# Half of the output projection moved from the third stage into the first, with group 0's qkv, the bias vectors and the first key loads in another order

## The chip, the cores and the metric

The kernel runs on one core of a Trainium2 chip. The metric is the device time of one execution in microseconds (us); lower is better. Of each kernel there are timed executions and one more under the hardware profiler, whose trace is shown here.

## The reference, cut to what matters

One layer of a hybrid decoder for a prompt of 2048 tokens and a sample group of 64 (8 sequences of 8 new tokens). All arrays are float32.

```
proj  = rms_norm(x) @ w_in              # 1024 -> q | k | v | r | k | v | three low-rank inputs
att   = dilated_attention(q, k, v)      # 8 heads x 64; three strided key sets, position bias
rw    = rwkv7_time_mix(proj[..., 1536:])   # 8 heads x 64; a state of 64 x 64 per head, token after token
h     = x + concat([att, rw], -1) @ w_out          # 1024 -> 1024
y     = h + relu(rms_norm(h) @ w_mlp1)**2 @ w_mlp2 # 1024 -> 4096 -> 1024
```

The rows 0 to 511 of `w_out` belong to attention (A), the rows 512 to 1023 to the recurrence (R). The projection is a sum of both halves, so either can be added first. The sample group reads 2048 cached keys and values for each of its eight sequences.

## The kernel before, in words

Every product with weights is done as three matmuls of rounded halves (hi x hi, hi x lo, lo x hi), so each operand is split by ScalarE (hi) and VectorE (lo = value - hi) first (`split`). Partitions hold features, columns hold tokens. All DMAs are issued from SP, in one queue, in order.

The order of each engine's instructions is fixed when the program is built: a planner simulates the program and takes, among what it believes ready, what has the best priority. Text order is the priority, except inside `with urgent()`, which puts its instructions ahead of all filler.

**Stage one** (`ph1`). Tokens are taken in four groups of 512, the 64 sample tokens with group 0. `norm1(g)` writes the normalised group as eight tile pairs nh, nl (one buffer each). `proj(g)` makes the recurrence's 15 column blocks (`rproj`, matmuls at L330) and stores them to xsD; `qkv(g)` makes the attention's six blocks (matmuls at L789) and stores qhD, qlD, khD, klD and vD. The recurrence runs in units of 256 tokens, the sample first, then units 0 to 7 (`core(unit(u))`), all urgent: small matmuls, a triangular solve on POOL, round trips through DRAM, then eight dependent chunks. Units 2g and 2g+1 need proj(g). Each unit's results go to DRAM as mixR. qkv(0) comes last, after all units, with a second `norm1(0)`:

```
proj(0, *nhl)
...
    if g + 1 < NG:
        proj(g + 1, *norm1(g + 1))      # qkv(g + 1) inside
for _ in qkv(0, *norm1(0)):
    pass
```

`bias_vectors` builds the position bias in DRAM: bvD holds, for each head, the bias by distance repeated for 128 partitions. It is advanced by one step after each block of proj(1).

**Stage two.** Attention over four pairs of heads. `kq_load(p)` loads a pair's keys and queries in twelve DMAs of 64 partitions x 2048 columns, `bias_load` its bias, `next_v` the values. A pair's three branches are merged and stored to DRAM as mixA.

**Stage three.** For eight chunks of 264 tokens, the output projection: `wo_panel` loads and splits a panel of 128 rows of w_out, `mix_panel` 128 rows of mixA or mixR, and each of eight output blocks takes 24 matmuls (L1431), the recurrence's panels 4 to 7 first. The residual x is loaded into h (L1421) and the sum added. The sample's attention is interleaved, two steps after each output block: it streams 42 MB of cached keys and values through four buffers of 512 KB. Its results, attS, are columns of the last chunk.

**Stage four.** The MLP (L1488, L1505) in two halves of the tokens.

Of the kernel before, what the change touches and what calls it, by code (L numbers as in the profile page):

```python
# [9 lines left out]
F32 = mybir.dt.float32  # L10
F32R = mybir.dt.float32r
# [19 lines left out]
def bc(ap, axis, n):  # L31
    a = ap.unsqueeze(axis)
    shape = list(a.shape)
    shape[axis] = n
    return a.broadcast_to(shape)
# [135 lines left out]
def _build(ctx, tc, nc, I, O, dbg, upto):  # L171
# [8 lines left out]
    def tt(out, a, b, op):  # L180
        V.tensor_tensor(out, a, b, op)  # L181
# [37 lines left out]
    xsD = dram.tile([15, P, T + NS], F32, name="xsD")  # L219
    mixA = dram.tile([4, P, T + NS], F32, name="mixA")  # L220
    mixR = dram.tile([4, P, T + NS], F32, name="mixR")


    rw = ph1.enter_context(pool(name="rw", bufs=1))
# [27 lines left out]
    def pj():  # L252
        return ppj.tile([P, 512], F32, name="pj", tag="pj")

    def split(src, hi, lo):
        act(hi, src, AF.Copy)
        tt(lo, src, hi.bitcast(F32), ALU.subtract)
# [200 lines left out]
    def bias_vectors():  # L458

        btab = c1.tile([33, 8], F32, name="btab")  # L460
        nc.sync.dma_start(out=btab, in_=I["btab"])
        bv1 = dram.tile([8, 3, 384], F32, name="bv1")

        def by_distance(src, n):
            oh = wp.tile([P, 512], F32, name="oh", tag="qn", bufs=3)
            nc.sync.dma_start(out=oh[:33, :n], in_=src)
            ps = pj()
            PE.matmul(ps[:8, :n], btab, oh[:33, :n], start=True, stop=True)
            sb = wp.tile([P, 512], F32, name="sb", tag="qn", bufs=3)
            act(sb[:8, :n], ps[:8, :n], AF.Copy)  # L470
            return sb

        for b in range(3):
            nc.sync.dma_start(out=bv1[:, b], in_=by_distance(I["oneh"][:, b], 384)[:8, :384])
            yield
        for h in range(0, 8, 4):
            nc.sync.dma_start(out=bvD[h:h + 4].rearrange("h p b n -> h p (b n)"), in_=bc(bv1[h:h + 4].rearrange("h b n -> h (b n)"), 1, P))
        for c in range(0, NSV, 512):
            n = min(512, NSV - c)
            nc.sync.dma_start(out=svD[:, :, c:c + n], in_=bc(by_distance(I["soneh"][:, c:c + n], n)[:8, :n], 1, 8))  # L480
            yield
# [208 lines left out]
            urgent.at, tc.cur_priority = tc.cur_priority, self.other  # L690

    AFTER = ((), (), (), ())

    def proj(g, nh, nl):

        other = qkv(g, nh, nl) if g else iter(())
        for i, j in enumerate((12, 13, 14, 4, 0, 8, 5, 1, 9, 6, 2, 10, 7, 3, 11)):
            rproj(g, j, nh, nl)  # L700
            if g == 1:
                next(bias, None)
            if i in AFTER[g]:
                next(other, None)
            if i == 12 and g + 1 < NG:
                sums(g + 1)
        for _ in other:
            pass

    def unit(g):  # L710
        st = new_unit()
# [35 lines left out]
    def sample_unit():  # L747
        st = new_unit()

        def padded(js, t):  # L750
            n = len(range(*js.indices(15)))
            c = rw3.tile([P, 3, NS], F32, name="xsc", bufs=1)[:, :n]
            nc.sync.dma_start(out=c, in_=xsD[js, :, T:].rearrange("j q t -> q j t"))
            G.memset(t, 0.0)
            for j in range(n):
                G.tensor_copy(t[:, j].rearrange("p (b i) -> p b i", i=C)[:, :, :8], c[:, j].rearrange("p (b i) -> p b i", i=8))
            return t

        st["lora"] = lora_prep(lambda t: padded(slice(12, 13), t.unsqueeze(1)))

        def xgate():
            x = rw3.tile([P, 3, UT], F32, name="xrkv")
            nc.sync.dma_start(out=x[:, 0, :NS], in_=xsD[13, :, T:])
            nc.sync.dma_start(out=x[:32, 1, :NS], in_=xsD[14, :32, T:])
            return x[:, 0, :NS], x[:32, 1, :NS]

        st["xgate"] = xgate
        preps(st, lambda p: padded(slice(p, p + 9, 4), rw3.tile([P, 3, UT], F32, name="xrkv")), True)
        return st
# [171 lines left out]
    urgent.at, tc.cur_priority = tc.cur_priority, tc.cur_priority + FILL  # L941
    with urgent():
        core(sample_unit(), UT, True, -1, lambda n: None)
    z = zt[core.count % NZ]
    G.memset(z[0:64, 0], 0.0)
    G.memset(z[64:128, 1], 0.0)
    for g in range(NG):
        for u in (2 * g, 2 * g + 1):
            with urgent():
                core(unit(u), UT, False, u, lambda n: None)  # L950
        if g + 1 < NG:
            proj(g + 1, *norm1(g + 1))
            if g + 2 == NG:
                nc.sync.dma_start(out=O["o_shift"], in_=sho)
    for _ in qkv(0, *norm1(0)):
        pass
    prj.close()

    ph1.close()
# [31 lines left out]

    evac.n = 0

    def kq_load(p):

        kq = kqs[p % 2]
        K = []
        for ty in range(2):
            rr = slice(ty * 64, ty * 64 + 64)
            kst = kq.tile([P, T], F32R, name=f"kst{ty}", tag="kq")  # L1000
            klo = kq.tile([P, T], F32R, name=f"klo{ty}", tag="kq")
            qst = kq.tile([P, T], F32R, name=f"qst{ty}", tag="kq")
            for dst, src, r0 in ((kst, khD, 0), (qst, qhD, 0), (kst, khD, 64), (qst, qlD, 64), (klo, klD, 0), (klo, klD, 64)):
                nc.sync.dma_start(out=dst[r0:r0 + 64].bitcast(F32), in_=src[p, rr])
            K.append((kst, klo, qst))
        return K

    def bias_load(p, b):
# [171 lines left out]
                yield  # L1180
            nc.sync.dma_start(out=mixA[p, :, cs], in_=ob[0][:, cs])

    ahead = {("kq", 0): kq_load(0)}
    for b in range(3):
        ahead["bias", 0, b] = bias_load(0, b)
    vq.append(next(vgen))
    wsel = at.tile([P, 4, P], F32R, name="wsel")
    wsel0 = at.tile([P, 4, P], F32, name="wsel0", tag="pts", bufs=4)
    nc.sync.dma_start(out=wsel0, in_=I["wsel"])
# [102 lines left out]

    NT = T + NS
    NC_ = 264
    woh = [None] * KT
    wol = [None] * KT

    def wo_panel(w, k):

        woh[k], wol[k] = w[:, 0:D], w[:, D:]  # L1300
        for o in range(0, D, 512):
            wr = we.tile([P, 512], F32, name="raw", bufs=3)
            nc.sync.dma_start(out=wr, in_=I["wo"][:, k, o:o + 512])
            split(wr, woh[k][:, o:o + 512], wol[k][:, o:o + 512])

    def mix_panel(pl, k, c0):

        mh = pl.tile([P, NC_], F32R, name="mh", bufs=5)
        ml = pl.tile([P, NC_], F32R, name="ml", bufs=5)
        src = (mixA if k < 4 else mixR)[k % 4]  # L1310
        n = min(NC_, (T if k < 4 else NT) - c0)
        mr = we.tile([P, 512], F32, name="mr", tag="raw", bufs=3)
        nc.sync.dma_start(out=mr[:, :n], in_=src[:, c0:c0 + n])
        split(mr[:, :n], mh[:, :n], ml[:, :n])
        if n < NC_:
            split(attS[:, k], mh[:, n:], ml[:, n:])
        return mh, ml
# [37 lines left out]
    attS = sat.tile([P, 4, NS], F32, name="attS")  # L1355

    kvs.append((sat, 2))
    for k in (4, 5):
        wo_panel(we.tile([P, 2 * D], F32R, name=f"wo{k}"), k)
    mixed = {}  # L1360
    for k in range(4, 8):
        mixed[k, 0] = mix_panel(we, k, 0)
    for _ in rest:
        pass
    ph2.close()
# [43 lines left out]
    with pool(name="wo2", bufs=1) as wo2, pool(name="pwo", bufs=4, space=PSUM, side="right") as pwo, pool(name="psa", bufs=1, space=PSUM) as psa, pool(name="pst", bufs=1, space=PSUM) as pst:  # L1409
        kvs.append((wo2, 2))  # L1410
        sample = sample_all(psa)
        for k in (6, 7, 0, 1, 2, 3):
            wo_panel(kqb.tile([P, T], F32R, name="wo", tag="kq"), k)
        tile_ = 0
        ends = [(i + 1) * P for i in range(8)] + [1088 + i * P for i in range(9)]
        order = (4, 5, 6, 7, 0, 1, 2, 3)
        for c0 in range(0, NT, NC_):
            if c0 + NC_ == NT:
                for _ in sample:
                    pass  # L1420
            nc.sync.dma_start(out=h[:, :, c0:c0 + NC_], in_=I["xh"][:, :, c0:c0 + NC_])  # L1421
            for k in order:
                if (k, c0) not in mixed:
                    mixed[k, c0] = mix_panel(we if k >= 4 else wo2, k, c0)
            for o in range(KT):
                ps = pwo.tile([P, 512], F32, name="pwo")
                i = 0
                for k in order:
                    mh, ml = mixed[k, c0]
                    for a, b in ((woh, mh), (woh, ml), (wol, mh)):  # L1430
                        PE.matmul(ps[:, :NC_], a[k][:, o * P:(o + 1) * P], b, start=(i == 0), stop=(i == 3 * KT - 1))  # L1431
                        i += 1
                tt(h[:, o, c0:c0 + NC_], ps[:, :NC_], h[:, o, c0:c0 + NC_], ALU.add)
                for _ in range(2):
                    next(sample, None)
            while tile_ < 17 and ends[tile_] <= c0 + NC_ < NT:
                square_sums(tile_, pst.tile([P, 512], F32, name="pst"), wo2)
                tile_ += 1
# [108 lines left out]
```

## Time and profile before

| | before |
|---|---|
| median of 3 runs | 3414.67 us (3407.58 to 3416.85) |
| profiled execution | 3415.77 us |
| its span, first to last instruction | 3414.0 us |
| mean granted TensorE clock | 0.974 of full speed |
| PE shown busy | 3209.2 us (94%) |
| VectorE, ScalarE, POOL busy | 50%, 39%, 12% |
| read from and written to DRAM | 286.2 and 79.3 MB |

PE is TensorE's matmuls, PEld its weight loads, DVE VectorE, ACT ScalarE, SPq the sequencer of SP that issues the DMAs. Lines such as L789 are lines of the kernel before. Matmuls overlap in the array, so a matmul's shown duration is longer than its distance to the next one.

### The profile page before, as it was taken

The page shows a single profiled execution, that of the slowest core. Times are in us where ns is not written, and L with a number is a line of the kernel's source. Part 1 is how long each engine was busy: PE and PEld are TensorE (multiplying, and loading weights), DVE is VectorE, ACT ScalarE, POOL GpSimd, SP SyncE. Part 2 cuts the span into 40 slices and gives each one's busy share as a digit, 9 for nine tenths or more (in the row PEclk, how much of TensorE's full clock was granted, in tenths as well). Part 3 has the DMA queues.
Part 4 walks back from the last instruction along what each step waited for, and adds up shares of the span by engine and source line. Part 5 has one row for each costly group of instructions (what it writes and reads, how often), then busy time and mean ns, then how long its engine had stood idle before and what let it go on. Part 6 is the DMA issues. An engine that isn't in the chain of part 4 may idle for free.

```text
span 3414.0 us, 60201 instructions
## 1 busy us (share of the span) xinstructions
PE 3209.2 (94%) x23646; PEld 2791.4 (82%) x23646; DVE 1713.4 (50%) x3951; ACT 1326.7 (39%) x3209; POOL 395.2 (12%) x713
## 2 busy tenths in 40 slices
PE   5959999999999979989899999999999999999999
PEld 5836877786788857878688899999999988888887
DVE  4635676677677525546554643333333633333333
ACT  4435564565455536657322322222222322222221
POOL 1003243342354100111000000000000000000000
PEclk9979999999999989999899999999999999999999
DMA  5445464465355495333776111111111211111112
GB/s 165 136 141 161 131 191 139 119 174 145 112 146 153 131 212 113 94 87 99 261 244 206 44 47 44 47 44 44 44 46 44 97 49 49 48 50 47 50 47 74
DMA packets 336968, 364.73 MB, mean 107 GB/s; under 512 B 112907, under 2 KB 226374, under 8 KB 333612
## 3 DMA queue, kind: packets, MB, share of 16 engines
q1 hardware_dynamic: 336684, 360.88, 36.5%
q8 instruction: 186, 3.05, 0.4%
q14 instruction: 98, 0.80, 0.1%
HBM read 286.20 MB, written 79.30 MB: 107 GB/s over the span
## 4 chain that ended last, share of the span: by engine, by line
PE 59%; DMA 6%; DVE 2%; SPq 1%; issue 1%; ACT 1%; POOL 1%; DVEq 0%; ACTq 0%; POOLq 0%
PE pm L1505 21%; PE pm L1488 21%; PE pwo L1431 4%; PE o L1091 2%; PE sc L1066 2%; PE pt L1084 2%; PE sc L1067 2%; PE pj L789 1%; DMA kst<-khD 1%; DMA vt<-vD 1%; DMA kv<-in_kc 1%; DMA mr<-mixA 1%; SPq L1421 1%; PE sc L1233 0%; DMA wD<-wh 0%
## 5 line engine op out<-in xcount | busy, mean ns | idle before, releaser
L184 ACT ACTIVATE wh<-wr 128x512 fp32r<-128x512 f32 (+1 forms) x472 | 294.3, 624 | 1027.5 <-PE pm L1505 582.3
L181 DVE TENSOR_TENSOR wl<-wr,wh 128x512 fp32r<-128x512 f32 (+1 forms) x472 | 325.9, 692 | 425.0 <-ACT wh L184 410.7
L1488 PE MATMUL pm<-mml,wh 128*128 128x512 f32 (+2 forms) x1280 | 452.5, 354 | 3.3 <-DVE mml L181 3.3
L1488 PE MATMUL pm<-mmh,wh 128*128 128x512 f32 (+2 forms) x1280 | 454.8, 356 | 0.4 <-ACT mmh L184 0.4
L1488 PE MATMUL pm<-mmh,wl 128*128 128x512 f32 (+2 forms) x1280 | 452.8, 354 | 0.0
L1505 PE MATMUL pm<-fh,wh 128*128 128x512 f32 (+2 forms) x1280 | 450.5, 355 | 0.0
L1505 PE MATMUL pm<-fh,wl 128*128 128x512 f32 (+2 forms) x1280 | 449.6, 353 | 0.0
L1505 PE MATMUL pm<-fl,wh 128*128 128x512 f32 (+2 forms) x1280 | 448.4, 352 | 0.0
L181 DVE TENSOR_TENSOR h<-pm,h 128x364 f32<-128x364 f32 (+1 forms) x320 | 190.5, 598 | 423.9 <-PE pm L1505 423.7
L1488 PEld LDWEIGHTS pm<-mml,wh 128*128 128x128 f32 x1280 | 241.0, 188 | 27.4 <-DVE mml L181 5.9
L1488 PEld LDWEIGHTS pm<-mmh,wl 128*128 128x128 f32 x1280 | 241.9, 189 | 22.5
L1505 PEld LDWEIGHTS pm<-fh,wl 128*128 128x128 f32 x1280 | 240.7, 188 | 22.4
L1488 PEld LDWEIGHTS pm<-mmh,wh 128*128 128x128 f32 x1280 | 241.4, 189 | 19.9 <-ACT mmh L184 0.9
L1505 PEld LDWEIGHTS pm<-fl,wh 128*128 128x128 f32 x1280 | 240.0, 188 | 21.5
L1505 PEld LDWEIGHTS pm<-fh,wh 128*128 128x128 f32 x1280 | 240.3, 188 | 19.2
L789 PE MATMUL pj<-wh,nh 128*128 128x256 f32 (+1 forms) x816 | 237.3, 292 | 7.5 <-ACT qn L184 3.5
L789 PE MATMUL pj<-wh,nl 128*128 128x256 f32 (+1 forms) x816 | 236.2, 290 | 1.0 <-DVE nl L181 0.9
L330 PE MATMUL pj<-nh,wh 128*128 128x512 f32 (+3 forms) x600 | 222.7, 375 | 13.2 <-ACT nh L184 9.9
L789 PE MATMUL pj<-wl,nh 128*128 128x256 f32 (+1 forms) x816 | 234.6, 288 | 0.0
L330 PE MATMUL pj<-nl,wh 128*128 128x512 f32 (+3 forms) x600 | 221.6, 370 | 3.9 <-DVE nl L181 3.8
L330 PE MATMUL pj<-nh,wl 128*128 128x512 f32 (+3 forms) x600 | 217.5, 365 | 0.0
L184 ACT ACTIVATE e<-e,st 128x256 f32<-128x256 f32 (+1 forms) x384 | 174.3, 455 | 106.3 <-DVE st L1069 104.4
(295 smaller groups left out, 6105.3 us busy)
## 6 DMA issues: line engine op xcount, KB each, us to landing
wr<-in_w SPq DMA_DIRECT2D x256, 256.0 KB
wr<-in_wr SPq DMA_DIRECT2D x120, 256.0 KB
wr<-in_wq SPq DMA_DIRECT2D x96, 256.0 KB
kv<-in_kc SPq DMA_DIRECT2D x40, 512.0 KB
kv<-in_vc SPq DMA_DIRECT2D x40, 512.0 KB
xsD<-xst SPq DMA_DIRECT2D x56, 256.0 KB
xrkv<-xsD SPq DMA_DIRECT2D x32, 384.0 KB
vt<-vD SPq DMA_DIRECT2D x48, 256.0 KB
```

Source lines behind the costliest of these rows:

```text
L181: V.tensor_tensor(out, a, b, op)
L184: S.activation(out, in_, func, bias=bias, scale=scale, **kw)
L330: PE.matmul(ps[:m, :n], a[:, k, :m], b[h * 4 + k][:, c0:c0 + n], start=(h == 0 and i == 0), stop=(h == 1 and i == 11))
L789: PE.matmul(out, a[h * 2 + k][:, i * P:i * P + m], b[:, k, :], start=(h == 0 and q == 0 and i % 2 == 0), stop=(h == 3 and q == 5 and (i % ...
L1066: PE.matmul(ps[:, c0:c0 + n], cols(qst, b, i, False), cols(kst, b, i, both), start=True, stop=False)
L1067: PE.matmul(ps[:, c0:c0 + n], cols(qst, b, i, False), cols(klo, b, i, both), start=False, stop=True)
L1084: PE.transpose(pt[:, y * P:(y + 1) * P], e[:, c0:c0 + P], ident)
L1091: PE.matmul(o[ty * 64:ty * 64 + 64, (i % 4) * P:(i % 4 + 1) * P], kv[:, ty * 64:ty * 64 + 64], ptss[ty][:, y * P:(y + 1) * P], start=fst, ...
L1421: nc.sync.dma_start(out=h[:, :, c0:c0 + NC_], in_=I["xh"][:, :, c0:c0 + NC_])
L1431: PE.matmul(ps[:, :NC_], a[k][:, o * P:(o + 1) * P], b, start=(i == 0), stop=(i == 3 * KT - 1))
L1488: PE.matmul(ps[:, :n], a[:, k], b[:, hf * 4 + k, c0:c0 + n], start=(hf == 0 and i == 0), stop=(hf == 1 and i == 11))
L1505: PE.matmul(ps[:, :n], a[:, f], b[:, c0:c0 + n], start=(i == 0), stop=(i == 11))
```

## The change: what it does

- `out_first`, at the end of stage one: the recurrence's half of the output projection, from mixR and panels 4 to 7 of w_out, plus the residual x, is stored to DRAM as hD. Five chunks of 512, 512, 512, 288 and 288 columns, 12 matmuls for each of eight output blocks. The weights stand in the tiles of nh and nl.
- Stage three loads hD into h in place of x and runs the attention's panels 0 to 3 alone: 12 matmuls for a block in place of 24.
- qkv(g) is written right after proj(g); qkv(0) after the sample's unit. The second norm1(0) is gone.
- bvD is written head by head, one head in a step; `bias_vectors` is advanced in proj(1) and proj(2).
- The first pair's keys and queries are loaded by quarters of the columns (48 DMAs for 12), after the first branch's bias and the first values.

```
+    hD = dram.tile([P, KT, T + NS], F32, name="hD")
...
-        for h in range(0, 8, 4):
-            nc.sync.dma_start(out=bvD[h:h + 4].rearrange("h p b n -> h p (b n)"), in_=bc(bv1[h:h + 4].rearrange("h b n -> h (b n)"), 1, P))
+        for h in range(8):
+            nc.sync.dma_start(out=bvD[h:h + 1].rearrange("h p b n -> h p (b n)"), in_=bc(bv1[h:h + 1].rearrange("h b n -> h (b n)"), 1, P))
+            yield
...
-            if g == 1:
+            if g in (1, 2):
                 next(bias, None)
...
+    def wo_parts(src, hi, lo):
+        wr = wp.tile([P, 4, P], F32, name="wr", tag="wr").rearrange("p a m -> p (a m)")
+        nc.sync.dma_start(out=wr, in_=src)
+        split(wr, hi, lo)
+
+    def out_first():
+        woh, wol = [], []
+        for k in range(4):
+            for lst, nm in ((woh, "nh"), (wol, "nl")):
+                lst.append([nt.tile([P, GT + NS], F32R, name=f"{nm}{2 * k + x}")[:, :512] for x in range(2)])
+            for x in range(2):
+                wo_parts(I["wo"][:, 4 + k, x * 512:x * 512 + 512], woh[k][x], wol[k][x])
+        for c0, n in ((0, 512), (512, 512), (1024, 512), (1536, 288), (1824, 288)):
+            parts = []
+            for k in range(4):
+                mr = wp.tile([P, 4, P], F32, name="wr", tag="wr").rearrange("p a m -> p (a m)")
+                nc.sync.dma_start(out=mr[:, :n], in_=mixR[k, :, c0:c0 + n])
+                mh = wp.tile([P, 4, P], F32R, name="wh", tag="wh", bufs=4).rearrange("p a m -> p (a m)")[:, :n]
+                ml = wp.tile([P, 4, P], F32R, name="wl", tag="wl", bufs=4).rearrange("p a m -> p (a m)")[:, :n]
+                split(mr[:, :n], mh, ml)
+                parts.append((mh, ml))
+            for o in range(KT):
+                xo = wp.tile([P, GT + NS], F32, name="xo", tag="xg", bufs=3)[:, :n]
+                nc.sync.dma_start(out=xo, in_=I["xh"][:, o, c0:c0 + n])
+                ps = pj()
+                i = 0
+                os_ = slice(o % 4 * P, o % 4 * P + P)
+                for k, (mh, ml) in enumerate(parts):
+                    for a, b in ((woh, mh), (woh, ml), (wol, mh)):
+                        PE.matmul(ps[:, :n], a[k][o // 4][:, os_], b, start=(i == 0), stop=(i == 11))
+                        i += 1
+                tt(xo, ps[:, :n], xo, ALU.add)
+                nc.sync.dma_start(out=hD[:, o, c0:c0 + n], in_=xo)
...
         core(sample_unit(), UT, True, -1, lambda n: None)
+    for _ in qkv(0, *nhl):
+        pass
...
-            proj(g + 1, *norm1(g + 1))
+            nhl = norm1(g + 1)
+            proj(g + 1, *nhl)
...
-    for _ in qkv(0, *norm1(0)):
-        pass
+            for _ in qkv(g + 1, *nhl):
+                pass
+    out_first()
     prj.close()
...
-    ahead = {("kq", 0): kq_load(0)}
-    for b in range(3):
+    ahead = {("bias", 0, 0): bias_load(0, 0)}
+    vq.append(next(vgen))
+    ahead["kq", 0] = kq_load(0, 4)
+    for b in range(1, 3):
         ahead["bias", 0, b] = bias_load(0, b)
-    vq.append(next(vgen))
...
-    for k in (4, 5):
-        wo_panel(we.tile([P, 2 * D], F32R, name=f"wo{k}"), k)
-    mixed = {}
-    for k in range(4, 8):
-        mixed[k, 0] = mix_panel(we, k, 0)
...
-            nc.sync.dma_start(out=h[:, :, c0:c0 + NC_], in_=I["xh"][:, :, c0:c0 + NC_])
-            for k in order:
-                if (k, c0) not in mixed:
-                    mixed[k, c0] = mix_panel(we if k >= 4 else wo2, k, c0)
+            nc.sync.dma_start(out=h[:, :, c0:c0 + NC_], in_=hD[:, :, c0:c0 + NC_])
+            mixed = [mix_panel(wo2, k, c0) for k in range(4)]
```

## Rows read from the trace of the kernel before

**Rows 1.** The page: busy time of each engine

```profile
PE 3209.2 (94%) x23646; PEld 2791.4 (82%) x23646; DVE 1713.4 (50%) x3951; ACT 1326.7 (39%) x3209; POOL 395.2 (12%) x713
```

**Rows 2.** The chain that ended last, by time: start us, duration us, what

```profile
1159.21 2.91 PE pj L789 x23
...
1538.18 5.29 DMA raw<-in_wo
...
1886.61 18.36 PE pwo L1431 x150
...
2035.80 47.79 PE pm L1488 x288
...
2750.56 43.95 PE pm L1505 x192
```

**Rows 3.** Windows: length, busy us (instructions) by engine, clock, DMA share, GB/s

```profile
205.00:246.00 41.00, 7.13 (x46) 3.42 (x45) 9.86 (x25) 7.06 (x19) 0.24 (x2) 0.60 0.36 128
...
914.00:1055.00 141.00, 137.83 (x1526) 119.76 (x1526) 106.72 (x212) 88.18 (x201) 50.20 (x80) 1.00 0.51 148
1055.00:1187.00 132.00, 123.63 (x1452) 111.03 (x1450) 77.75 (x150) 64.87 (x137) 49.88 (x73) 0.97 0.42 118
...
1209.00:1231.00 22.00, 2.30 (x7) 1.58 (x7) 0.30 (x2) 0.20 (x2) 0.00 (x0) 0.59 1.02 237
```

**Rows 4.** Windows of line L789 alone (three), then of L330 alone (one)

```profile
914.00:1055.00 141.00, 80.35 (x573) 71.53 (x574) 1.00 0.51 148
1055.00:1187.00 132.00, 81.50 (x606) 73.83 (x604) 0.97 0.42 118
1187.00:1209.00 22.00, 15.80 (x120) 15.54 (x120) 0.92 0.90 229
...
775.00:914.00 139.00, 93.35 (x358) 65.05 (x359) 0.98 0.49 138
```

**Rows 5.** Timeline of SP's queue: start us, duration us, what

```profile
194.94 9.96 SPq L477 DMA_DIRECT2D bvD<-bv  x2
205.00 21.99 SPq L313 DMA_DIRECT2D wr<-in_wr  x1
...
1236.13 0.59 SPq L1004 DMA_DIRECT2D kst<-khD  x1
```

**Rows 6.** Waits between 150 and 260 us: total us, times, longest us

```profile
ACT wh L184 <- DMA wr<-in_wr: 35.1, 4, 30.3
...
PE pj L468 <- DMA oh<-in_soneh: 27.5, 1, 27.5
```

**Rows 7.** Timelines of PE and DVE around the end of stage one

```profile
1186.66 0.60 PE L611 MATMUL cs<-ident,yc 128*128 128x128 f32 x4
...
1230.54 0.29 DVE L1069 CUSTOM_DVE_ANT_0 e<-sc,bt 128x128 f32<-128x128 f32 x1 [37.25 <-DMA bt<-bvD]
```

**Rows 8.** Windows of line L1431 alone: PE, PEld, clock, DMA share, GB/s

```profile
1640.00:1709.00 69.00, 31.73 (x240) 30.29 (x240) 0.80 0.93 307
1709.00:1873.00 164.00, 121.84 (x897) 112.01 (x898) 1.00 0.70 226
1873.00:1922.00 49.00, 49.00 (x397) 48.30 (x396) 1.00 0.12 32
```

**Rows 9.** Window of line L1233 alone

```profile
1709.00:1873.00 164.00, 17.32 (x240) 5.57 (x240) 1.00 0.70 226
```

**Rows 10.** Groups of instructions: busy us, mean ns, idle before and its releaser

```profile
L184 ACT ACTIVATE wh<-wr 128x512 fp32r<-128x512 f32 (+1 forms) x472 | 294.3, 624 | 1027.5 <-PE pm L1505 582.3 <-PE pm L1488 252.4 <-DMA wr<-in_wr 77.6
L181 DVE TENSOR_TENSOR wl<-wr,wh 128x512 fp32r<-128x512 f32 (+1 forms) x472 | 325.9, 692 | 425.0 <-ACT wh L184 410.7 <-PE pj L330 11.9 <-PE ms L381 1.0
...
L812 POOL TENSOR_TENSOR qrs<-qss,mhalf 128x20 f32<-128x20 f32 x16 | 58.3, 3642 | 66.1 <-DVE qss L178 45.0 <-DVE mean L178 21.1
```

**Rows 11.** DMA issues: line and count, KB each

```profile
h<-in_xh SPq DMA_DIRECT2D x8, 1056.0 KB
...
mr<-mixR SPq DMA_DIRECT2D x32, 132.0 KB
```

More of the change, by code (lines that the diff above doesn't have):

```diff
@@ L690, in __exit__ @@
             urgent.at, tc.cur_priority = tc.cur_priority, self.other
-    AFTER = ((), (), (), ())
     def proj(g, nh, nl):
-        other = qkv(g, nh, nl) if g else iter(())
         for i, j in enumerate((12, 13, 14, 4, 0, 8, 5, 1, 9, 6, 2, 10, 7, 3, 11)):
             rproj(g, j, nh, nl)
-            if g == 1:
+            if g in (1, 2):
                 next(bias, None)
-            if i in AFTER[g]:
-                next(other, None)
             if i == 12 and g + 1 < NG:
                 sums(g + 1)
-        for _ in other:
-            pass
+    def wo_parts(src, hi, lo):
+        wr = wp.tile([P, 4, P], F32, name="wr", tag="wr").rearrange("p a m -> p (a m)")
+        nc.sync.dma_start(out=wr, in_=src)
+        split(wr, hi, lo)
@@ L951, in _build @@
         if g + 1 < NG:
-            proj(g + 1, *norm1(g + 1))
+            nhl = norm1(g + 1)
+            proj(g + 1, *nhl)
             if g + 2 == NG:
                 nc.sync.dma_start(out=O["o_shift"], in_=sho)
-    for _ in qkv(0, *norm1(0)):
-        pass
+            for _ in qkv(g + 1, *nhl):
+                pass
+    out_first()
     prj.close()
@@ L992, in _build, with kq_load @@
     evac.n = 0
-    def kq_load(p):
+    def kq_load(p, steps=1):
         kq = kqs[p % 2]
[L997 to L1005, printed above, removed]
+        K = [[kq.tile([P, T], F32R, name=f"{nm}{ty}", tag="kq") for nm in ("kst", "klo", "qst")] for ty in range(2)]
+        for i in range(steps):
+            cs = slice(i * T // steps, (i + 1) * T // steps)
+            for ty in range(2):
+                rr = slice(ty * 64, ty * 64 + 64)
+                kst, klo, qst = K[ty]
+                for dst, src, r0 in ((kst, khD, 0), (qst, qhD, 0), (kst, khD, 64), (qst, qlD, 64), (klo, klD, 0), (klo, klD, 64)):
+                    nc.sync.dma_start(out=dst[r0:r0 + 64, cs].bitcast(F32), in_=src[p, rr, cs])
         return K
@@ L1294, in _build @@
     NC_ = 264
-    woh = [None] * KT
-    wol = [None] * KT
+    woh = [None] * 4
+    wol = [None] * 4
     def wo_panel(w, k):
@@ L1309, in mix_panel @@
         ml = pl.tile([P, NC_], F32R, name="ml", bufs=5)
-        src = (mixA if k < 4 else mixR)[k % 4]
-        n = min(NC_, (T if k < 4 else NT) - c0)
+        n = min(NC_, T - c0)
         mr = we.tile([P, 512], F32, name="mr", tag="raw", bufs=3)
-        nc.sync.dma_start(out=mr[:, :n], in_=src[:, c0:c0 + n])
+        nc.sync.dma_start(out=mr[:, :n], in_=mixA[k, :, c0:c0 + n])
         split(mr[:, :n], mh[:, :n], ml[:, :n])
@@ L1411, in _build @@
         sample = sample_all(psa)
-        for k in (6, 7, 0, 1, 2, 3):
+        for k in range(4):
             wo_panel(kqb.tile([P, T], F32R, name="wo", tag="kq"), k)
@@ L1415, in _build @@
         ends = [(i + 1) * P for i in range(8)] + [1088 + i * P for i in range(9)]
-        order = (4, 5, 6, 7, 0, 1, 2, 3)
         for c0 in range(0, NT, NC_):
@@ L1427, in _build @@
                 i = 0
-                for k in order:
-                    mh, ml = mixed[k, c0]
+                for k, (mh, ml) in enumerate(mixed):
                     for a, b in ((woh, mh), (woh, ml), (wol, mh)):
-                        PE.matmul(ps[:, :NC_], a[k][:, o * P:(o + 1) * P], b, start=(i == 0), stop=(i == 3 * KT - 1))
+                        PE.matmul(ps[:, :NC_], a[k][:, o * P:(o + 1) * P], b, start=(i == 0), stop=(i == 11))
                         i += 1
```

## The prediction

> **What bounds the kernel now.** I read the page first. PE is busy for 94% of the span [rows 1], and the MLP, from 1922 us on, is a closed train: 288 matmuls of about 363 columns in 47.79 us, 192 of 512 columns in 43.95 us [rows 2]. That is 166 and 229 ns from start to start, a line of 0.42 ns per column, so 288 columns cost about 134 ns. The output projection's 264 columns run at 18.36 us / 150 = 122 ns when nothing disturbs them [rows 2]. The change does not touch the MLP; the time is decided before 1922 us.
>
> Then the windows of the first stage. Between 914 and 1187 us PE is shown busy for 261 of 273 us [rows 3], yet it runs only 573 + 606 of the qkv matmuls (L789) there [rows 4]; at 126 ns each (2.91 us / 23 [rows 2]) that is 149 us. The other 124 us belong to two units' small matmuls and to gaps that pipelined ends cover up. Between 205 and 246 us PE does almost nothing: 7 us busy, clock 0.60 [rows 3]. The queue says why: the two 2.3 MB writes of bvD are issued at 194.94, and the weight load behind them takes 21.99 us to issue [rows 5]. The waits agree: PE stood 27.5 us for a small load of soneh, ACT 30.3 us for one weight panel [rows 6].
>
> The end of stage one: unit 7's last transposes are at 1186.66 us, and group 0's qkv, the filler, goes on to 1209 [rows 4, 7]. The first softmax instruction of attention is at 1230.54, released by a bias load that stands behind the key loads in the queue [rows 7]. In between the DMA share is 1.02 and PE does 2.3 us of work in 22 [rows 3].
>
> Last, output projection and sample attention, 1640 to 1922 us: 240, 897 and 397 of the 1536 matmuls in three stretches, with 307, 226 and 32 GB/s [rows 8]. In the middle stretch, 164 us, 240 of the sample's score matmuls run [rows 9], 40 for a batch, so six batches, 27.3 us each.
>
> **The change part by part.**
>
> *Recurrence half into stage one (out_first).* 3 chunks x 8 x 12 = 288 matmuls of 512 columns at 229 ns = 66.0 us, and 2 x 8 x 12 = 192 of 288 columns at 134 ns = 25.7 us: 91.7 us of PE. Below, a part falls into the gaps of units 6 and 7 (the 124 us); above, they cost 91.7 in full. I take the full price, because today the filler already outlasts the recurrence by 22 us: there is no lack of filler for those gaps now, and the order of PE's queue is fixed when the program is built. The weights need 8 loads and splits (ACT 624, DVE 692 ns each [rows 10], some 6 us, pipelined), but the second norm1(0) goes, which leaves qkv(0) waiting for about 8 us: -3. Each chunk begins with four loads of mixR and four splits, into as many buffers as one chunk uses, so the next chunk's splits follow the last matmuls of the one before: about 4 us exposed on the two last chunks, 2 on the three earlier ones, +14.
>
> On what "busy" is worth: the Trainium skill, Perfetto Trace Analysis, section Identifying the Most-Contended Engine, says that matmul busy share is not a good measure of distance from the roofline. The trace agrees (261 us shown busy, 149 us of filler). By that rule a part of the new matmuls would be free, which is rival B.
>
> *Group 0's qkv first, bvD by head.* Over the 41 us of the hole PE gets qkv(0)'s 720 matmuls (88 us at 122 ns) to run, and no 2.3 MB write stands in the queue. The bytes of bvD stay; eight pieces of 0.6 MB, each some 4 us of queue (the two blocked it for 10 + 22 us [rows 5]), lie between weight panels that are double-buffered. Bounds 0 and -41; I take -38. The price is that proj(1) to proj(3) come after qkv(0), about 88 - 38 = 50 us later, and unit 6 needs proj(3), which ends at 914 now (358 of its 360 matmuls are before that [rows 4]). Units 6 and 7 then run from 964 instead of 914; at today's 273 us they end near 1237. That is inside the PE sum, so I add nothing. Four instructions of POOL at 3.6 us each (L812 [rows 10]) move with qkv(0) in front of the solves of the sample and unit 0; these units are early by then, so I leave their 15 us out. Out_first brings 108 issues on SP, at 0.4 us some 43 us of a queue that has 273.
>
> Stage one: 91.7 - 3 + 14 - 38 = +65, so the last projection matmul comes near 1274 instead of 1209.
>
> *Handover.* Today 22 us pass from 1209 to 1231. After it, khD has long been written, the key tiles reuse memory that unit 7 releases, and the first quarter (twelve loads of 128 KB, 1.5 MB, at 237 GB/s about 7 us) and the first bias pair can land while out_first's last two chunks run. 48 issues in place of 12 at about 0.5 us each (L1004 [rows 5]) are 24 us of queue, as long as the 6.3 MB take anyway. Bounds 0 and -22; I take -17. The second pair's key loads come in one piece as before, so the later stall on V stays.
>
> The Trainium skill, DMA: Bandwidth & Descriptors, section Bandwidth, asks for transfers of 1 MiB or more and speaks against quarters and heads. This trace moves 307 GB/s with pieces of 132 to 1056 KB in flight together [rows 8, 11]; the rule would take back perhaps 7 us of the handover (an estimate from that page's table).
>
> *Stage two.* Panels 4 and 5 of wo and four mixR panels are no longer loaded during pair 3; one such load stands 5.29 us in the chain [rows 2]: -5, bounds 0 and -10.
>
> *Stage three.* 768 matmuls of 122 ns go: -94 us if PE alone decided. But the 240 matmuls done before 1709 used mixR, while mixA of pair 3 was awaited [rows 8]; that cover is gone (I leave about 40). After 1709 there remain 728 x 0.122 = 89 us, and the sample's share, 164 - 897 x 0.122 = 55 us: 1853. By bytes: 21 + 37 + 2 = 60 MB now, less 3.8 of mixR and 1 of wo, 55 MB; at 300 GB/s 183 us, 1823, and after it the last chunk (96 x 0.122 = 12 us, with its panel some 15). The two limits lie so close that they will hinder each other: 1858 instead of 1922, -64. Bounds: -94, and -34 if the batches keep 27.3 us (rival C).
>
> Sum: +65 - 17 - 5 - 64 = -21 on the profiled execution's 3415.8 (1.8 above its span, 1.1 above the median shown): **3394 us**.
>
> **The rivals.** *B, the gaps take more.* Half of the 91.7 us falls into the 124 us that hold units 6 and 7, and stage three gains 75: +65 - 46 - 17 - 5 - 75 = -78, 3338; with a third of it, 3353. I put it at 3350. For it: the count of starts [rows 3, 4]. Against it: the gaps have had filler to take and did not.
>
> *C, the sample keeps its pace.* If loads and softmax, not PE, set 27.3 us a batch, the sample still ends at 1873 and the last chunk at 1888: -34 instead of -64, 3424. For it: kv buffers are few and 0.5 MB each. Against it: the projection's matmuls alone are 897 x 0.122 = 109 of those 164 us [rows 8].
>
> *D, the other side: the keys stand before the last chunks.* The queue issues in order. If the key loads (6.3 MB, 26 us at 237 GB/s) are issued as soon as unit 7 ends, the loads of mixR and xh and the stores of hD for the last two chunks wait behind them; xo has three buffers, so PE stops. Price: 26 us, and PE restarts at the low clock, as it did in the window at 0.59 [rows 3], where 100 matmuls of 134 ns cost 13 us more: +39, 3433. It decides as soon as more than half of the keys come first. For it: after unit 7 the last two chunks (2.4 MB in, 2.4 out, 1.2 of mixR) and the keys need 12 MB together, 50 us at today's rate. Against it: the order is planned, and out_first is written first.
>
> **How the numbers follow.** A, the forecast, 0.50, its own range 3370 to 3418; B 0.18; C 0.15; D 0.17. Some 0.3% (10 us) is what a measurement of this kernel tells from no change. A gives 0.38 faster, 0.11 same, 0.01 slower; B 0.18 faster; C 0.01, 0.08, 0.06; D 0, 0.03, 0.14. Together 0.57, 0.22, 0.21. The range leaves out the lower half of B and the upper third of D: 3350 to 3436.
>
> **What would show it.** Right: no window near 200 us with PE under half busy, L789 there; the last projection matmul near 1274; the first softmax instruction within 6 us of it; 768 projection matmuls in stage three, their last near 1858 + 43 (stage one and handover shift it by 48, stage two by -5); then the MLP as before, 1491 us. Wrong: a projection that ends before 1250 (B), batches still 27 us apart (C), PE idle between unit 7's end and the last chunk with key loads in the queue (D), or bvD's pieces that still stop the weight panels.

## The result, and the profile after

The change takes 3455.36 us (median of 4, 3453.06 to 3459.05) where the kernel before takes 3411.34 (3407.58 to 3416.85): a ratio of 1.0129, 95% interval 1.011 to 1.0148. It is slower by 44 us; 3394 was forecast, and 3436 was the upper end of the range. The profiled execution took 3455.72 us with a span of 3453.9, against 3414.0 before.

The page of the changed kernel, engine line and clock: PE's share has not moved [rows 1], and of the 40 slices of 86 us the clock is below 0.9 in those from 1209 to 1381, from 1727 to 1813 and from 1900 to 1986 us.

```profile
PE 3244.6 (94%) x23354; PEld 2797.9 (81%) x23354; DVE 1720.9 (50%) x3953; ACT 1324.5 (38%) x3189; POOL 393.8 (11%) x713
PEclk9999999999999988999989799999999999999999
```

Windows of the changed kernel (length; busy us of PE, PEld, DVE, ACT, POOL; clock; DMA share; GB/s). The first is the stretch in which PE stood still before [rows 3].

```profile
205.00:246.00 41.00, 39.71 (x405) 33.47 (x403) 26.11 (x56) 23.67 (x57) 6.16 (x7) 0.98 0.38 110
...
1016.00:1283.00 267.00, 246.04 (x2335) 206.59 (x2334) 152.05 (x288) 108.43 (x238) 82.99 (x142) 0.94 0.55 157
1283.00:1310.00 27.00, 16.09 (x106) 15.39 (x106) 6.51 (x14) 1.77 (x4) 0.00 (x0) 0.87 0.67 199
1310.00:1313.00 3.00, 1.19 (x9) 0.88 (x7) 0.76 (x2) 0.00 (x0) 0.00 (x0) 0.95 0.69 210
```

The hole is gone: 39.7 of 41 us busy. Yet unit 7 ends late. Its last transposes, which were at 1186.66 [rows 7], are the second half of this group (the changed kernel's line L613, from its first to its last start); it is followed by the first softmax of attention on DVE.

```profile
L613 PE MATMUL cs<-ident,yc x8: 270/347/476, 1260.1 to 1282.6; 128*128 128x128 f32 x8
```
```profile
1313.07 0.28 DVE L1102 CUSTOM_DVE_ANT_0 e<-sc,bt 128x128 f32<-128x128 f32 x1
```

Windows of one line alone (length, PE, PEld, clock, DMA share, GB/s): group 0's qkv (L819), the last projection of the recurrence (L331), out_first (L735), and the output projection of stage three (L1455).

```profile
145.00:326.00 181.00, 103.77 (x720) 91.77 (x720) 0.96 0.52 141
...
888.00:1016.00 128.00, 93.26 (x360) 65.50 (x360) 0.97 0.41 126
...
1163.00:1253.00 90.00, 73.87 (x288) 53.38 (x288) 0.98 0.58 172
1253.00:1310.00 57.00, 30.29 (x192) 28.57 (x192) 0.82 0.50 152
...
1735.00:1776.00 41.00, 6.25 (x48) 6.04 (x48) 0.79 0.82 275
1776.00:1908.00 132.00, 88.81 (x624) 82.03 (x624) 0.94 0.81 261
1908.00:1961.00 53.00, 11.91 (x96) 11.76 (x96) 0.72 0.58 188
```

Group 0's qkv ends at 326, proj(3) at 1016 (914 before, [rows 4]), out_first at 1310, the output projection at 1961 (1922 before). By stage the 39.9 us between the two spans are:

| stretch | before | after | difference | forecast |
|---|---|---|---|---|
| to the last projection matmul of stage one | 1209 | 1310 | +101 | +65 |
| from there to the first softmax | 22 | 3 | -19 | -17 |
| stage two | 409 | 423 | +14 | -5 |
| stage three to the last output projection | 283 | 225 | -58 | -64 |
| MLP | | | +1 | 0 |

Stage three gained what it was to gain; stage one, and to a smaller part stage two, went wrong.

### The profile page after: what moved, and what is told of

The parts are those of the page before. It is cut to its first block, busy times and chain, and to the rows that moved or that the text cites. A ratio compares the mean times of both kernels' runs of the same rounds, so it can differ in the third digit from the quotient of the medians.

```text
span 3453.9 us, 59766 instructions
## 1 busy us (share of the span) xinstructions
PE 3244.6 (94%) x23354; PEld 2797.9 (81%) x23354; DVE 1720.9 (50%) x3953; ACT 1324.5 (38%) x3189; POOL 393.8 (11%) x713
## 4 chain that ended last, share of the span: by engine, by line
PE 58%; DMA 6%; DVE 1%; SPq 1%; issue 1%; POOL 1%; ACT 1%; DVEq 0%; ACTq 0%
PE pm L1529 21%; PE pm L1512 21%; PE pwo L1455 3%; PE o L1124 2%; PE sc L1099 2%; PE pt L1117 2%; PE sc L1100 2%; DMA kv<-in_kc 1%; PE pj L735 1%; DMA vt<-vD 1%; DMA kst<-khD 1%; SPq L1038 1%; PE pj L819 1%; DMA wD<-wh 1%; PE ax L1311 1%
## 5 line engine op out<-in xcount | busy, mean ns | idle before, releaser
L184 ACT ACTIVATE wh<-wr 128x512 fp32r<-128x512 f32 (+2 forms) x492 | 305.2, 622 | 1034.7 <-PE pm L1529 582.3
L181 DVE TENSOR_TENSOR wl<-wr,wh 128x512 fp32r<-128x512 f32 (+2 forms) x492 | 337.4, 687 | 428.0 <-ACT wh L184 422.6
L1512 PEld LDWEIGHTS pm<-mml,wh 128*128 128x128 f32 x1280 | 242.0, 189 | 25.6 <-DVE mml L181 3.9
L819 PE MATMUL pj<-wh,nh 128*128 128x256 f32 (+1 forms) x816 | 237.8, 293 | 4.0 <-ACT qn L184 1.7
L819 PE MATMUL pj<-wl,nh 128*128 128x256 f32 (+1 forms) x816 | 238.2, 292 | 0.7 <-DVE wl L181 0.5
L819 PE MATMUL pj<-wh,nl 128*128 128x256 f32 (+1 forms) x816 | 237.6, 292 | 0.0
L331 PE MATMUL pj<-nh,wh 128*128 128x512 f32 (+3 forms) x600 | 220.2, 369 | 14.3 <-ACT nh L184 11.9
L331 PE MATMUL pj<-nl,wh 128*128 128x512 f32 (+3 forms) x600 | 220.5, 368 | 2.2 <-DVE nl L181 2.1
L331 PE MATMUL pj<-nh,wl 128*128 128x512 f32 (+3 forms) x600 | 219.5, 368 | 0.0
```

What stands on the lines that cost most here:

```text
L184: S.activation(out, in_, func, bias=bias, scale=scale, **kw)
L331: PE.matmul(ps[:m, :n], a[:, k, :m], b[h * 4 + k][:, c0:c0 + n], start=(h == 0 and i == 0), stop=(h == 1 and i == 11))
L819: PE.matmul(out, a[h * 2 + k][:, i * P:i * P + m], b[:, k, :], start=(h == 0 and q == 0 and i % 2 == 0), stop=(h == 3 and q == 5 and (i % ...
L1512: PE.matmul(ps[:, :n], a[:, k], b[:, hf * 4 + k, c0:c0 + n], start=(hf == 0 and i == 0), stop=(hf == 1 and i == 11))
```

## The experiments

Two theories stood against each other for stage one. **Work:** the sum of PE's work sets its end, wherever a piece stands in the order. **Order:** unit 7 ends so long after proj(3), and what stands ahead of proj(3) delays it in full. Each kernel below ran in 4 timed executions unless another number is given, beside the kernel before; the ratios are to that. In the table (times in us) the ends of proj(3) and of unit 7 are last starts on PE, the first softmax is the first one on DVE; "stage two" goes from there to the first score matmul of the sample, "stage three" on to the last output projection matmul.

| kernel | time | proj(3) | unit 7 | first softmax | stage two | stage three |
|---|---|---|---|---|---|---|
| before | 3411 to 3414 | 914 | 1187 | 1231 | 409 | 283 |
| the change | 3455 | 1016 | 1283 | 1313 | 423 | 225 |
| a, qkv(0) last | 3462 | 918 | 1167 | 1341 | 402 | 227 |
| b, no out_first | 3456 | 1015 | 1244 | 1255 | 424 | 285 |
| d, reorder only | 3470 | 1037 | 1255 | 1291 | 401 | 284 |
| g, qkv(0) by itself | 3462 | 1016 | 1283 | 1314 | 423 | 229 |
| c, bias only | 3388 | 913 | 1160 | 1216 | 397 | 282 |
| p, keys only | 3422 | 911 | 1184 | 1205 | 428 | 285 |
| f, bias and keys | 3402 | 914 | 1162 | 1218 | 406 | 282 |
| e, whole keys | 3466 | 1014 | 1284 | 1340 | 402 | 228 |
| i, smaller chunks | 3475 | 1012 | 1296 | 1321 | 429 | 224 |
| q, half left out | 3339 | 912 | 1161 | 1217 | 398 | 229 |

**a: the change, with group 0's qkv last again.**

```
-    for _ in qkv(0, *nhl):
-        pass
     z = zt[core.count % NZ]
...
+    for _ in qkv(0, *norm1(0)):
+        pass
     out_first()
```

> The changed kernel with one thing undone: group 0's qkv stands after all units again, with the second norm1(0), and out_first behind it. Theory order (units 4 and 6 wait for proj(2) and proj(3), which qkv(0) pushes back): proj(3) ends near 880 instead of 1016, unit 7 near 1155 instead of 1283, the last projection matmul of stage one near 1265 instead of 1310; time about 3412, 43 below the change. Theory work (stage one lasts as long as PE's sum, in any order): the last projection matmul stays within 10 us of 1310, plus 8 for norm1(0); time 3455 to 3465.

Measured: 3461.71 us, ratio 1.0138 (1.0116 to 1.016). Unit 7 ends 116 us earlier than in the change, and nothing comes of it: group 0's qkv ends at 1209, out_first begins at 1228, and its 480 matmuls take 110 us with no unit beside them. The window behind 1209 in this kernel:

```profile
1209.00:1340.80 131.80, 100.19 (x482) 81.69 (x482) 38.84 (x66) 15.55 (x28) 0.00 (x0) 0.92 0.72 216
```

So with this order work decides, though the last projection matmul, at 1338, lies 10 us beyond what that theory gave, and out_first costs more than its full price: 110 us, and 19 more before its first matmul.

**b: the change without out_first** (the residual is read from xh again and stage three does both halves).

```
-    out_first()
     prj.close()
```

> The changed kernel without out_first: all 24 matmuls of a block in stage three as before, but qkv(0) first, bvD by head, first keys by quarters. Theory order: proj(3) still ends near 1000 and unit 7 near 1265, nothing behind it; the first softmax instruction near 1270 (before 1230); time near 3450. Theory work: 92 us of matmuls less in stage one, no hole: the stage ends near 1165 to 1175, first softmax near 1180; time near 3360.

Measured: 3456.46 us, 1.013 (1.0103 to 1.0157). With 480 matmuls fewer in stage one it is no faster than the change, as order said, while work gave 3360. Two windows of this kernel show where the time is: from proj(3) to unit 7's end PE is busy for 174 of 229 us, and then stands idle.

```profile
1015.00:1244.00 229.00, 174.34 (x1960) 148.63 (x1958) 117.79 (x234) 94.91 (x214) 79.55 (x142) 0.81 0.48 123
1244.00:1254.80 10.80, 1.04 (x3) 0.58 (x2) 1.38 (x2) 0.00 (x0) 0.47 (x1) 0.50 0.64 182
```

Group 3's qkv ends at 1152 in b; after it nothing is left for PE beside the chain of units 6 and 7, and the clock of the whole stretch is 0.81. Before, PE was busy there for 261 of 273 us, at 0.97 and more [rows 3].

**d: before, with nothing but group 0's qkv moved to the front.**

```
+    for _ in qkv(0, *nhl):
+        pass
     z = zt[core.count % NZ]
...
-            proj(g + 1, *norm1(g + 1))      # qkv(g + 1) inside
+            nhl = norm1(g + 1)
+            proj(g + 1, *nhl)
+            for _ in qkv(g + 1, *nhl):
+                pass
```

> The kernel before with one part of the change: qkv(0) after the sample's unit, qkv(g) after proj(g), no second norm1(0); bvD in two writes and keys in one piece as before. Theory order: unit 7 ends near 1265 or later, time 3445 to 3470. Theory work: stage one ends near 1200, time 3400 to 3410 (8 us of norm1(0) saved, and a hole at the bvD writes wherever they now fall).

Measured: 3469.55 us, 1.0166 (1.0147 to 1.0185): the reorder alone costs 55 us. proj(3) ends 123 us later, unit 7 68 (10 us short of what order gave), and the keys find nothing beside them: of the 36 us from there to the first softmax PE is busy for 3.

```profile
1255.00:1290.80 35.80, 2.84 (x10) 1.85 (x8) 1.38 (x2) 0.00 (x0) 1.15 (x2) 0.50 0.93 196
```

**g: the change, with group 0's qkv ahead of the sample's unit**, so that it runs with no chain beside it.

```
+    for _ in qkv(0, *nhl):
+        pass
     urgent.at, tc.cur_priority = tc.cur_priority, tc.cur_priority + FILL
     with urgent():
         core(sample_unit(), UT, True, -1, lambda n: None)
-    for _ in qkv(0, *nhl):
-        pass
```

> The change, but group 0's qkv is emitted ahead of the sample's recurrence unit, so it runs without a chain beside it. It should then take some 90 to 110 us instead of 181 (145 to 326), so the projections end earlier: proj(1) near 410 to 425 instead of 490, while the sample's unit and unit 0 end some 90 us later than in the change (306 and 438). Order theory (unit 7 is set by when the projections of its group are done and by the chain from there, the early units' lead is lost waiting): the later early units cost nothing as long as unit 4 still waits for proj(2) and unit 6 for proj(3); the end of stage one moves by what proj(3) moves, 0 to -40 us, and the time is 3415 to 3458. Work theory (the sum of TensorE's work sets the end whatever stands where): 3450 to 3460, no change. If the early lead of the units was worth something, it is slower: 3480 and more.

Measured: 3461.64 us, 1.0153 (1.0138 to 1.0168), just above what either theory gave. Group 0's qkv ends at 259 instead of 326; proj(1) ends 56 us earlier than in the change, proj(2) 36, proj(3) not at all; the sample's unit ends 99 us later, unit 0 83, unit 3 55, unit 5 already 15 us earlier, unit 7 at the same time. The stretch that ends with proj(3) is full in both kernels; this is g's row, and that of the change differs by 2 us:

```profile
761.00:1016.00 255.00, 242.47 (x2344) 194.20 (x2344) 171.68 (x341) 140.76 (x321) 78.14 (x145) 0.98 0.50 141
```

So neither the early lead of the units nor the slow pace of a filler beside them matters by itself. Ahead of proj(3) it is the sum of the work that counts: the whole of group 0's qkv now stands there, at either place. Both theories are needed, one on each side of proj(3).

**c: before, with bvD written by head and nothing else.**

```
-        for h in range(0, 8, 4):
-            nc.sync.dma_start(out=bvD[h:h + 4]...
+        for h in range(8):
+            nc.sync.dma_start(out=bvD[h:h + 1]...
+            yield
...
-            if g == 1:
+            if g in (1, 2):
```

> The kernel before with one part of the change: bvD written head by head, bias_vectors advanced in proj(1) and proj(2). If the hole at 205 to 246 us is the two 2.3 MB writes, it goes and the units run some 35 us earlier: 3370 to 3385. If the writes only move to another place of the queue and stop it there: within 10 us of 3411. Both theories of stage one say the same here; the run prices the part.

Measured: 3388.24 us (3386.35 to 3394.59), 0.9929 (0.9909 to 0.995): **faster than both kernels**, by 0.7% or some 24 us against the change's 44 the other way. Windows of this kernel: the hole, the stretch from proj(3) to unit 7, and from there to the first softmax.

```profile
205.00:246.00 41.00, 34.61 (x225) 25.62 (x225) 25.63 (x54) 22.41 (x53) 0.35 (x3) 0.92 0.67 181
...
913.00:1160.00 247.00, 227.62 (x2572) 201.98 (x2571) 157.50 (x307) 126.63 (x277) 92.47 (x147) 0.97 0.45 127
1160.00:1215.80 55.80, 36.56 (x261) 35.01 (x260) 11.57 (x20) 13.92 (x25) 5.76 (x3) 0.79 0.97 256
```

The hole closes, but proj(3) ends at 913 as before: only the units move up (unit 0 by 38 us, unit 7 by 27). Group 0's qkv even ends 7 us later, at 1215, while the keys, at a DMA share of 0.97, pass beside its last panels. The first softmax follows it at once:

```profile
1215.78 0.29 DVE L1070 CUSTOM_DVE_ANT_0 e<-sc,bt 128x128 f32<-128x128 f32 x1 [9.06 <-PE sc L1068]
```

So the 22 us between the two before [rows 3] are gone. By the traces 15 us are gained at the first softmax and 12 in stage two; what the latter are, no run shows.

**p, f, e: the first keys.** p is before with the quarters alone, f has c's bias and quarters issued in the order 2, 3, 4, 1, with the first values behind them, e is the change with twelve whole loads.

```
+        for cs in parts:                     # p: quarters 1, 2, 3, 4; f: 2, 3, 4, 1
...
-    ahead["kq", 0] = kq_load(0, 4)           # e
+    ahead["kq", 0] = kq_load(0)
```

> The kernel before with one part of the change: first bias, first values, then the first pair's keys by quarters. Here group 0's qkv still ends stage one, and the first quarter of the keys is group 0's, the last to be written. Expected: within 10 us of 3411; if 48 issues block the queue in front of the last qkv panels: 3420 to 3440.

> The kernel before with bvD by head and the first pair's keys by quarters in the order 1, 2, 3, 0, so that only the quarter which group 0's qkv writes last is loaded behind it. Expected by both theories: at or below the 3388 of bvD by head alone, 3370 to 3388; the queue blocked by 48 issues would show as 3390 to 3410.

> The changed kernel with the first pair's keys in twelve whole loads again (first bias and first values still ahead of them). If the quarters buy the early start: the first softmax instruction, 1313 in the change, comes 15 to 20 us later, without the gap from 1335 to 1347, and the time is 5 to 10 us above the change's 3455. If the 48 issues (24 us of SP's queue) only delay the biases and values behind them: 3445 to 3455.

Measured: p 3422.05 us (10 executions), 1.0028 (1.0017 to 1.0038); f 3401.87 (6 executions), 0.9971 (0.9959 to 0.9983); e 3465.69, 1.0164 (1.0147 to 1.0181). In p the first softmax comes 25 us earlier than before and stage two lasts 19 longer: ScalarE stands 14.6 us for the load of a constant behind the 48 issues (see below, *Stage two*). The 9 us that p loses lie within its expected 10. f missed its 3370 to 3388: it starts stage two 2 us later than c, needs 9 us more for it, and is 14 slower. So by themselves the quarters bring nothing. In the change they keep rival D away: with whole loads PE's last 24 matmuls of out_first stand still. Waits of e between 1300 and 1345 us (total, times, longest):

```profile
DVE xo L181 <- DMA xo<-in_xh: 32.3, 2, 28.8
...
PE pj L735 <- DVE xo L181: 24.8, 1, 24.8
```

The residual's loads (xo) stand behind key loads; out_first ends at 1339 instead of 1310, the first softmax comes 26 us later where 15 to 20 were expected, and 10 us of it are left at the end, since stage two is then 21 us shorter.

**i: the change, with the chunks of out_first cut so that less remains behind unit 7.**

```
-        for c0, n in (..., (1536, 288), (1824, 288)):
+        for c0, n in (..., (1536, 256), (1792, 128), (1920, 192)):
```

> The changed kernel with out_first's chunks 512, 512, 512, 256, 128 and 192 columns in place of 512, 512, 512, 288 and 288: one third less stands behind unit 7's last store. If the end of stage one is set by unit 7 and the chunk behind it (order): the last projection matmul, 1310, comes 6 to 10 us earlier, time 3445 to 3450. If it is set by PE's sum (work): the same or some us later, 3455 to 3462.

Measured: 3475.34 us, 1.0182 (1.0165 to 1.0199). Both expectations missed. The tail behind unit 7 is 22 us instead of 27, but unit 7 ends 13 us later, and its profiled execution (3467.20) lies 8 us under the median, so only some 12 us of the 20 can be read from the trace. Six chunks take 576 matmuls where five take 480, for the same columns, and they are shown busy for 120 us where the change's are for 104. Whether that is what delays unit 7 is not shown.

**q: c, with the recurrence's half of the output projection left out of stage three altogether.**

```
-        order = (4, 5, 6, 7, 0, 1, 2, 3)
...
+            mixed = [mix_panel(wo2, k, c0) for k in range(4)]
```

> The bias-only kernel (3388) with the recurrence's half of the output projection left out of stage three altogether: the sum that leaves is incomplete, the time tells what stage three alone gains when that half is done elsewhere at no cost. If the gain of stage three in the change (-58 us) does not depend on what stage one did to it: 3388 - 58 to 64 = 3324 to 3330. If the last batches are held by loads that the change had placed elsewhere, less: -34 (the sample keeping its old pace of 27.3 us a batch), 3354.

Measured: 3339.49 us, 0.979 (0.9773 to 0.9806), 48.8 us below c, which is between the two expectations. In the trace stage three is 53 us shorter than in c, stage two the same. So stage three's gain hardly depends on what happened to stage one (53 us here, 57 from c to the change), and some 50 us is all that out_first pays back; in a, where only out_first and the quarters are added to c, it costs 125 us at the first softmax.

## Why the prediction was wrong

The step of the prediction that failed is the price of putting group 0's qkv first: "about 88 - 38 = 50 us later", "they end near 1237. That is inside the PE sum, so I add nothing". proj(3) came 102 us later, not 50, and unit 7 at 1283, not 1237, which put the end of stage one 36 us beyond the forecast. Three kernels split the +101 us at the end of stage one into the three terms of my sum:

| step | end of stage one's PE work | measured | forecast |
|---|---|---|---|
| bvD by head (before to c) | 1208 to 1215 | +7 | -38 |
| qkv(0) first, quarters (c to b) | 1215 to 1244 | +28 | 0 |
| out_first (b to the change) | 1244 to 1310 | +66 | +103 |

*The hole.* I credited its 38 us to the filler. It went to the units, which had not been the last thing ([rows 4, 7]); proj(3) did not move. It is worth some 24 us all the same, 15 of them in the handover: unit 7 ends 27 us earlier, the first key load goes out 4 us after its last store as before (1167 instead of 1196), and the keys land beside the filler's last panels. In the change that same handover was to be hidden under out_first, so the sum held these 15 us twice (in -38 and in -17), and they were there once.

*The reorder.* That unit 6 waits for proj(3) can be read from the queue: its last inputs are loaded from xsD after proj(3)'s last block is stored there. The first two lines are of the kernel before, the others of the change (lines between them left out):

```profile
918.18 0.34 SPq L346 DMA_DIRECT2D xsD<-xst  x1
...
936.15 1.24 SPq L728 DMA_DIRECT2D xrkv<-xsD  x1
```
```profile
1018.72 0.34 SPq L347 DMA_DIRECT2D xsD<-xst  x1
...
1021.48 0.37 SPq L758 DMA_DIRECT2D xrkv<-xsD  x1
```

Before, 18 us lie between store and load: proj(3) was not what unit 6 waited for last, and had that much slack. In the change it is 3 us (in c, 2): proj(3) now sets the units' pace. The prediction took the 273 us behind proj(3) for units 6 and 7 alone; in the trace before, unit 4's last transposes come at 927, unit 5's at 1021 and unit 6's at 1111, so more than three units stood there.

Behind proj(3) stand the rest of unit 5 and units 6 and 7, a chain of 218 to 229 us with little beside it (d, b) and 247 to 273 with filler (c, before). Group 0's qkv was cheap filler for it. Moved ahead of proj(3), where PE is busy for 240 us or more of 255, its 720 matmuls delay proj(3) by no less than their length (102 us; 88 at 122 ns each, and 104 shown busy beside the units), and the chain behind proj(3) then runs with PE at 174 of 229 us. A sum over the stage does not see that a piece was moved from the one side of this point to the other. Of the 124 us that I held for units and gaps, the text said "there is no lack of filler for those gaps now": true before, and the change itself made the lack.

*out_first.* It fell into the slack that the reorder had made, which is why it cost 66 and not 103: part of rival B's mechanism, with another cause. That is also why b and the change take the same time: out_first adds 58 us at the first softmax in the change, and stage three (-60) gives them back. The costs don't add: against c, the reorder with the quarters alone costs 68 us (b), out_first with the quarters alone 73 (a), all together 67. With no unit beside it (a) it takes 110 us, and 19 ahead of them, where I had 103 in all; and behind unit 7 there remain 27 us in the change, since the last chunks need unit 7's own output. No run has out_first without the quarters and without the reorder, so 73 is not the price of out_first alone.

*Stage two.* I had -5 for loads that go away, and gave 48 issues "24 us of queue" at no cost. They run from 1291.5 to 1335, 44 us, among out_first's last loads and stores, and what stands behind them comes late: above all wsel, a constant that ScalarE copies once at the start of attention, issued at 1337.20. ScalarE's order is fixed when the program is built, so its next softmax instructions wait with it, TensorE waits for ScalarE, and VectorE for TensorE's scores. Waits of the changed kernel between 1255 and 1350 us, then the line of DVE's timeline, then PE's window in the hole, with a clock of 0.61:

```profile
ACT wsel L184 <- DMA wsel<-in_wsel: 14.2, 1, 14.2
...
PE o L1124 <- ACT pts L184: 9.2, 1, 9.2
```
```profile
1347.24 0.42 DVE L1102 CUSTOM_DVE_ANT_0 e<-sc,bt 128x256 f32<-128x256 f32 x1 [12.68 <-PE sc L1100]
```
```profile
1334.00:1347.00 13.00, 4.29 (x24) 3.30 (x25) 0.55 (x4) 4.71 (x14) 0.00 (x0) 0.61 0.91 240
```

b, p, g and i, with quarters in the same order, show the same hole behind the same load (12 to 14 us each), and stage two of 423 to 429 us. In a, whose keys are issued from 1178 us on, and in e, where they come whole, ScalarE has wsel before the first softmax; there is no such hole, and stage two takes 402 us, near the forecast; c, d and f have no such hole either (397 to 406 us). The hole is 13 of the 20 us between; the rest is open. No run moves wsel ahead of the keys.

The Trainium skill, DMA: Bandwidth & Descriptors, section Bandwidth, asks for transfers of 1 MiB or more. No run here tests size alone: p is 9 us slower with keys in pieces of 128 KB instead of 512, but with another order of the queue, and c is 24 us faster with eight bias writes of 0.6 MB instead of two of 2.3, but with another shape of the write (last section).

*Right:* the size of stage three (-58 for -64, and -53 in q); the handover (3 us, forecast within 6); the MLP; no window near 200 us half idle. Rival D did not come, though e shows that only the quarters kept it away.

*Right in size, less so in mechanism:* stage three. Rival C gave -34 for a sample that keeps its pace, and it nearly does: from the third batch to the eighth the first score matmuls come 25.6 us apart, 26.0 before. The projection now runs ahead of it, and the last chunk, at 1949, waits for the sample's end. Of the -58 us, 36 are projection matmuls that no longer stand behind the sample (48 us before, 12 now), which is C's term; the sample itself, from 1736, is 22 us shorter, 11 of them between its second and third batch. That these came on top was not foreseen by C; A's -64 was right by its number more than by its path.

The Trainium skill, Perfetto Trace Analysis, section Identifying the Most-Contended Engine, holds matmul busy share for a poor measure of distance from the roofline. This case agrees: the share is 94% in both kernels, 44 us apart. What it hid was which idle time had work to fill it, and that was to be read from what releases unit 7, not from a share.

## What to carry to other kernels

Where a latency-bound chain and filler share an engine, find the last piece of filler that the chain waits for (here proj(3)): work ahead of it delays the chain in full once the slack there is used up (18 us here), work behind it costs little up to the chain's own length (proj(3) to unit 7: 247 us in c with group 0's qkv beside the chain, 229 in b without). Moving a piece across that point is a change by itself, to be priced even when the stage's sum stays the same. And try the parts one by one: of the four edits here one gave 24 us, and the three others together took 67.

## What the runs showed of the hardware

Two broadcast writes held what stood behind them in the queue far beyond their own issue. They are of 2.3 MB each and took 9.96 us, and the load behind them 21.99 [rows 5]. In c the same bytes go out at the same place, 195 us, as eight pieces of 0.6 MB, and the loads and stores between them are issued in less than 1 us each. SP's timeline of c:

```profile
195.43 1.82 SPq L477 DMA_DIRECT2D bvD<-bv  x3
197.35 0.91 SPq L346 DMA_DIRECT2D xsD<-xst  x1
...
199.25 0.64 SPq L477 DMA_DIRECT2D bvD<-bv  x1
199.98 0.68 SPq L313 DMA_DIRECT2D wr<-in_wr  x1
...
205.65 6.46 SPq L477 DMA_DIRECT2D bvD<-bv  x4
212.22 0.78 SPq L346 DMA_DIRECT2D xsD<-xst  x1
```

I had allowed 4 us of queue for each piece; four of them in a row took 6.46 us. In the changed kernel all eight go out at 372 to 379 us, and no hole follows there either. The edit changes more than the size: a write's outermost dimension is four heads before and, in c, one head of 128 partitions. In the traces' DMA records the packets of these writes (4608 bytes each) are under way four at a time before, from 196.4 to 242.0 us, about as long as the hole; in c up to some sixteen at a time, from 196.8 to 220.2; in d, with the old writes at another place, again four at a time, from 373.7 to 419.4. So the number of packets under way at once goes with the hole, and the size need not be its cause; no run changes one of the two alone.

The granted clock was 0.50, the lower of its two levels, where PE was shown busy for 3 of 36 us (d), and 0.61 in the hole of the change. It was 0.81 where PE was busy for 174 of 229 us (b), but 0.92 in a's window behind 1209, with the same share (100 of 132). So the busy share of a stretch does not by itself give its clock.
